# A decoder block with mixed attention and recurrence: narrow score products in pairs, output weights split once, padded value rows, and keys split in two steps

## The chip, the cores and the metric

The kernel runs on one core of one Trainium2 chip. The core has a matrix engine (PE, TensorE, with its weight loads listed apart as PEld), a vector engine (DVE), an activation engine (ACT), a general engine (POOL, GpSimd), a queue engine that starts most DMAs (SP), and 16 DMA engines. Engines run side by side and wait for each other through semaphores; each works through its own instructions in the order in which they stand. The metric is the device time of one execution in microseconds (us), as a median over runs.

## What is computed

One decoder layer over 1024 tokens of width 1024, all in float32. Shortened, with what matters here:

```python
h = h + 0.5 * swiglu(rms_norm(h, ffn1_norm), ffn1_w_gu, ffn1_w_down)
h = h + hybrid_mixer(rms_norm(h, mix_norm), w_in, ..., w_out)
h = h + 0.5 * swiglu(rms_norm(h, ffn2_norm), ffn2_w_gu, ffn2_w_down)
return rms_norm(h, final_norm)

def hybrid_mixer(h, ...):                       # two groups of heads side by side
    o_nsa = nsa_group(...)                      # 8 heads of 64, two key groups
    o_hg = hgrn2_group(...)                     # 4 heads of 128, chunks of 64 tokens
    return concatenate([o_nsa, o_hg]) @ w_out

# hgrn2_group, per chunk and head: a gated linear recurrence
decay = exp(where(tril, b[t] - b[s], NEG))      # b: running sum of log gates
a = einsum('td,tsd,sd->ts', q, decay, k)
o = a @ v + (q * exp(b)) @ state

# nsa_group, per head: three softmaxes with a linear distance penalty, mixed by sigmoid gates
o = g0 * (p_c @ v_c) + g1 * (p_sel @ v_s) + g2 * (p_win @ v_w)
```

`v_c` holds 63 compressed positions per key group; `p_sel` runs over all causal keys (16 blocks of 64 exist and 16 are chosen), `p_win` over a window of 512.

## The kernel before

The float32 products of the dense parts are made of three float32r products: each operand is split into a rounded part and a remainder (`split`, lines 150 to 157: the rounded part on POOL or ACT, the remainder on DVE), and `mm3` (159) or `gemm_tm_steps` (717) multiply high by high, high by low and low by high. Smaller products of the recurrence stay in plain float32; such a product is two passes on PE.

The program goes through these stages, with times from the span's start: the first feed-forward part (0 to about 660 us), the mixer (660 to 1430), the second feed-forward part and the final norm (to the end). A tile framework gives each engine its order and its waits; code that yields (`dense` generators) is interleaved by hand with the rest, so that dense products stand between the dependent steps on PE.

**The recurrence** (`hgrn_unit`, 802, and the loop of `body` at 1406). For each of four heads and two halves of 512 tokens (8 units) the products of one head's two units are interleaved with the projections of the next head (`hgrn_proj`, 769). A unit makes the intra-chunk scores `A` level by level: `score` (811 to 816) multiplies `k` and `q` for four pairs of chunks, 128x128 each, into one PSUM bank; then DVE multiplies parts of `q` and `k` by gate products (832, 833), and the entries that belong to the level are taken over into `A`: the diagonal by a product with the identity (823), levels 0 to 4 by masked copies (837), each for two 64x64 diagonal blocks apart, levels 5 and 6 by copies on ACT (841). That is 8 score rounds per unit, 4 products each. Line 870 multiplies `A` by `v`.

**Compressed keys and values** (`compress`, 902) run in the same stage before the first head's units. `vcm`, the compressed values (977), has 63 rows.

**Attention** (1457 to 1490): for each block of 128 queries (`qb`) and each of two key groups (`g`), `att_soft` (1082) makes, for four heads, scores against the window keys, all keys and the compressed keys (1101, 1102), a minimum of the scaled negative scores by one DVE instruction (1107), exponentials on ACT (1142) and a scaling on POOL (1146). `att_pv` (1150) transposes the probabilities block by block (1175), splits them (1177 on ACT, 1178 on DVE) and multiplies them by the values (1166), the compressed block last, with 63 rows. Dense fillers run beside it: query projections (`att_proj_q`, 1004) in the first half, and in the second half the output product of the first half's tokens (`wout`, 1196). Query projections evacuate their bank in two steps per head pair, ACT (1024) and DVE (1025). `att_kv` (1061) splits the keys of one half for both groups: ACT copies (1078), DVE copies (1079) and DVE subtractions (1080). It is called once before the first half and once before the second (1456).

**The output weights** `w_out` are read in four column quarters (`cq`). `wpages` (301) loads a quarter in four pages and splits each (POOL and DVE); it is called four times in `wout` and once more for the first quarter of the second half's tokens (1485). `wo_pages` (435) does the same for the other three quarters of the second half (1516).

Of the kernel before, what the change touches and what calls it, by code (L numbers as in the profile page):

```python
# [9 lines left out]
F32 = mybir.dt.float32  # L10
# [61 lines left out]
class Net:  # L72
# [15 lines left out]
    def consts(self, ctx):  # L88
# [5 lines left out]
        self.ident = c.tile([128, 128], F32, name="ident")  # L94
        nc.vector.tensor_scalar(self.ident[:], it, 0.0, None, op0=OP.is_equal)
# [205 lines left out]
    def wpages(self, name, key):  # L301

        src = self.wsrc(name, key)
        h, l = [], []
        for kp in range(4):
            raw = self.ap.tile([128, 2, 256], F32, name=self.nm("wr"), tag="kr", bufs=4)
            self.nc.sync.dma_start(out=raw[:], in_=src[:, 2 * kp:2 * kp + 2])
            th, tl = (self.qp.tile([128, 2, 256], F32R, name=self.nm("wq"), tag="qa", bufs=16) for _ in range(2))
            self.split(th[:], tl[:], raw[:])
            h += [th[:, 0, :], th[:, 1, :]]  # L310
            l += [tl[:, 0, :], tl[:, 1, :]]
        return h, l

# [120 lines left out]

    def wo_pages(self, pool, cq):

        raw = self.up_raw(pool, "w_out", cq)
        h, l = [], []
        for kp in range(4):
            th, tl = (pool.tile([128, 4, 128], F32R, name=self.nm("wp"), tag="wp", bufs=16)[:].rearrange("p a b -> p (a b)")  # L440
                      .rearrange("p (k c) -> p k c", k=2) for _ in range(2))
            self.split(th, tl, raw[kp // 2][:, kp % 2 * 2:kp % 2 * 2 + 2, :])
            h += [th[:, 0, :], th[:, 1, :]]
            l += [tl[:, 0, :], tl[:, 1, :]]
        return h, l
# [291 lines left out]
    def mixer_consts(self, tp):  # L737
# [10 lines left out]
        nc.vector.tensor_tensor(out=xf, in0=xf, in1=up, op=OP.mult)  # L748
        self.lev = []
        for l in range(5):  # L750
            m = 1 << l
            nc.vector.tensor_scalar(up, xf, float(m), None, op0=OP.is_ge)
            k = c.tile([128, 128], U8, name=f"lev{l}")
# [48 lines left out]
    def hgrn_unit(self, p, t, half, states, mo):  # L802
# [8 lines left out]
        def score():  # L811
            b = self.bank("b")
            for c in range(4):
                s = slice(c * 128, c * 128 + 128)
                mm(b[:, s], k[:, s], q[:, s], start=True, stop=True)  # L815
            return b[:].rearrange("p (c t) -> p c t", c=4)

        blk = [(slice(o, o + 64), slice(None), slice(o, o + 64)) for o in (0, 64)]
        nc.gpsimd.memset(A[64:128, :, 0:64], 0.0)
        b = score()  # L820
        nc.vector.tensor_tensor(out=q[:], in0=q[:], in1=f[:], op=OP.mult)
        for x in blk:
            nc.vector.tensor_tensor(out=A[x], in0=b[x], in1=self.ident[x[0], None, x[2]].to_broadcast([64, 4, 64]), op=OP.mult)
        F, o = f[:], 0
        for l in range(7):
            m = 1 << l
            n = 512 // (2 * m)
            b = score()
# [6 lines left out]
            if m < 32:  # L835
                for x in blk:
# [65 lines left out]
    def compress(self, p, hg, sp, raw):  # L902
# [12 lines left out]
        self.vcm = sp.tile([64, 2, 128], F32R, name="vcm")  # L915
# [22 lines left out]
        for s in range(2):  # L938
# [29 lines left out]
            else:  # L968
# [6 lines left out]
                hi = self.vcm[:63, :, :64]  # L975
                nc.vector.tensor_copy(out=hi, in_=b3)
                nc.vector.tensor_tensor(out=self.vcm[:63, :, 64:], in0=b3, in1=hi.bitcast(F32), op=OP.subtract)
# [83 lines left out]
    def att_kv(self, p, half, pa=None):  # L1061
# [5 lines left out]
        for g in range(2):  # L1067
# [146 lines left out]
def body(ctx, tc, ins, out):  # L1214
# [177 lines left out]
    if True:  # L1392
# [9 lines left out]
        with cw:  # L1402
            with ExitStack() as ch:
                hg = pool(ch, "hg")
                steps = net.compress(ap_, hg, sp, Y["c"])
                for hh in range(5):
# [5 lines left out]
                    for _ in steps:  # L1412
                        next(dense, None)
                    for _ in dense:
                        pass
# [223 lines left out]
```

## Time and profile before

| | |
|---|---|
| median of 3 runs | 2064.36 us (2063.22 to 2068.18) |
| the profiled execution: its time | 2073.11 us |
| the profiled execution: its span, first to last instruction | 2071.4 us |
| mean granted clock of TensorE in it | 0.989 |
| stage 755 to 1000 us (recurrence) | PE busy 243.68 of 245 us |
| stage 1054 to 1376 us (attention) | PE busy 307.26 of 322 us, DVE 262.31 |
| DMA of the whole span | 273.31 MB, mean 132 GB/s |

The rows quoted below are of four kinds. A row of the timeline gives the start, the duration, the engine, the line and operation, the tiles written and read, and, in brackets, how long the engine had been idle and what ended that wait; "x16" stands for 16 like instructions that follow each other. A row of a group gives a line, an engine, an operation, its shapes and its count, then busy time and the mean duration of one in ns, then the idle time in front of it. A row by stretches gives the stretch and its length, the busy time of PE, PEld, DVE, ACT and POOL with their counts, the clock granted to TensorE (1.00 is full), the share of the DMA engines and GB/s. The page's rows give totals. For a product, "128*63 128x64" is a weight load of 63 columns from 128 rows, and 64 columns streamed over 128 rows.

### The profile page before, as it was taken

The page shows a single profiled execution, that of the slowest core. Times are in us where ns is not written, and L with a number is a line of the kernel's source. Part 1 is how long each engine was busy: PE and PEld are TensorE (multiplying, and loading weights), DVE is VectorE, ACT ScalarE, POOL GpSimd, SP SyncE. Part 2 cuts the span into 40 slices and gives each one's busy share as a digit, 9 for nine tenths or more (in the row PEclk, how much of TensorE's full clock was granted, in tenths as well). Part 3 has the DMA queues.
Part 4 walks back from the last instruction along what each step waited for, and adds up shares of the span by engine and source line. Part 5 has one row for each costly group of instructions (what it writes and reads, how often), then busy time and mean ns, then how long its engine had stood idle before and what let it go on. Part 6 is the DMA issues. An engine that isn't in the chain of part 4 may idle for free.

```text
span 2071.4 us, 30307 instructions
## 1 busy us (share of the span) xinstructions
PE 2023.3 (98%) x10382; PEld 1694.9 (82%) x10382; DVE 1454.0 (70%) x2953; ACT 773.8 (37%) x1619; POOL 531.2 (26%) x632
## 2 busy tenths in 40 slices
PE   8999999999999999999999899999999999999998
PEld 6888888887787889989877688788888888887886
DVE  7977778658766655666458888865867777557677
ACT  5533333313324222212267567645433333323233
POOL 2223223223321001000146444521211222113221
PEclk9999999999999999999989999999999999999999
DMA  5346666267664211100100111152436666247663
GB/s 183 117 134 212 201 231 218 72 217 223 214 193 161 69 57 32 31 27 28 39 18 22 31 47 45 43 179 102 137 116 228 211 205 208 86 143 257 208 193 140
DMA packets 143610, 273.31 MB, mean 132 GB/s; under 512 B 16064, under 2 KB 37600, under 8 KB 143456
## 3 DMA queue, kind: packets, MB, share of 16 engines
q1 hardware_dynamic: 137312, 258.25, 38.2%
q10 hardware_dynamic: 6144, 13.12, 1.7%
q8 instruction: 82, 1.34, 0.3%
q14 instruction: 72, 0.59, 0.1%
HBM read 195.30 MB, written 76.02 MB: 131 GB/s over the span
## 4 chain that ended last, share of the span: by engine, by line
PE 83%; DVE 8%; issue 4%; ACT 2%; DMA 1%; POOL 1%; SPq 0%; ACTq 0%; DVEq 0%; POOLq 0%
PE b L161 15%; PE b L163 15%; PE b L162 15%; PE b L671 6%; PE b L669 6%; PE b L670 6%; PE b L1166 3%; PE b L1175 3%; PE b L815 2%; PE b L725 2%; PE b L724 2%; PE b L726 2%; PE b L1102 1%; PE b L1101 1%; DVE P L1107 1%
## 5 line engine op out<-in xcount | busy, mean ns | idle before, releaser
L161 PE MATMUL b<-xT,wp 128*128 128x512 f32 x1196 | 467.7, 391 | 6.9 <-ACT pp L539 5.6
L162 PE MATMUL b<-xT,wp 128*128 128x512 f32 x1196 | 466.3, 390 | 0.0
L163 PE MATMUL b<-xT,wp 128*128 128x512 f32 x1196 | 465.9, 390 | 0.0
L157 DVE TENSOR_TENSOR dw<-dr,dw 128x512 fp32r<-128x512 f32 x308 | 239.4, 817 | 115.0 <-ACT dw L155 107.2
L161 PEld LDWEIGHTS b<-xT,wp 128*128 128x128 f32 x1196 | 225.1, 188 | 56.4 <-issue 6.0
L162 PEld LDWEIGHTS b<-xT,wp 128*128 128x128 f32 x1196 | 225.2, 188 | 47.1 <-DVE xT L352 0.4
L163 PEld LDWEIGHTS b<-xT,wp 128*128 128x128 f32 x1196 | 225.1, 188 | 46.9
L669 PE MATMUL b<-dw,dw 128*128 128x512 f32 x616 | 242.5, 394 | 7.7 <-DVE dw L157 5.9
L671 PE MATMUL b<-dw,dw 128*128 128x512 f32 x616 | 241.0, 394 | 0.6 <-DVE dw L157 0.4
L670 PE MATMUL b<-dw,dw 128*128 128x512 f32 x616 | 240.9, 391 | 0.0
L155 ACT ACTIVATE dw<-dr 128x512 fp32r<-128x512 f32 x154 | 96.6, 630 | 272.2 <-PE b L669 200.8
L153 POOL TENSOR_SCALAR dw<-dr 128x512 fp32r<-128x512 f32 x154 | 112.9, 735 | 297.8 <-PE b L671 207.8
L155 ACT ACTIVATE wp<-ws 128x512 fp32r<-128x512 f32 x148 | 93.3, 632 | 255.7 <-PE b L162 244.6
L1146 POOL TENSOR_SCALAR P<-P,sm,gate 128x64 f32<-128x64 f32 (+8 forms) x192 | 129.3, 687 | 127.2 <-DVE sm L1144 90.3
L669 PEld LDWEIGHTS b<-dw,dw 128*128 128x128 f32 x616 | 116.4, 189 | 35.5 <-issue 10.3
L671 PEld LDWEIGHTS b<-dw,dw 128*128 128x128 f32 x616 | 116.0, 189 | 29.2 <-DVE dw L157 5.2
L157 DVE TENSOR_TENSOR wp<-ws,wp 128x512 fp32r<-128x512 f32 x148 | 110.1, 745 | 40.1 <-ACT wp L155 40.0
L670 PEld LDWEIGHTS b<-dw,dw 128*128 128x128 f32 x616 | 116.5, 189 | 23.6
L155 ACT ACTIVATE wp<-wr 128x512 fp32r<-128x512 f32 x115 | 72.2, 628 | 156.5 <-PE b L162 128.4
L1142 ACT ACTIVATE P<-P,sm 128x64 f32<-128x64 f32 (+8 forms) x192 | 114.7, 599 | 35.1 <-DVE sm L1107 33.2
L460 POOL TENSOR_TENSOR ws<-wr 128x512 f32<-128x512 f32 x37 | 50.3, 1358 | 299.8 <-DVE wp L157 246.6
L157 DVE TENSOR_TENSOR wp<-wr,wp 128x512 fp32r<-128x512 f32 (+1 forms) x155 | 109.7, 715 | 16.5 <-ACT wp L155 14.2
(293 smaller groups left out, 4016.3 us busy)
## 6 DMA issues: line engine op xcount, KB each, us to landing
dr<-hs SPq DMA_DIRECT2D x242, 256.0 KB, 2.9
wr<-in_ffn_w_gu_dram SPq DMA_DIRECT2D x82, 512.0 KB, 4.0
hs<-hk SPq DMA_DIRECT2D x140, 256.0 KB, 3.8
hs<-wd SPq DMA_DIRECT2D x88, 256.0 KB, 2.8
wd<-in_ffn_w_down_dram SPq DMA_DIRECT2D x84, 256.0 KB, 3.4
dr<-in_ffn_w_down_dram SPq DMA_DIRECT2D x62, 256.0 KB, 3.9
wr<-in_w_in_dram SPq DMA_DIRECT2D x18, 512.0 KB, 4.1
wr<-in_w_out_dram SPq DMA_DIRECT2D x20, 256.0 KB, 3.0
```

The costliest lines, as they stand in the source:

```text
L153: nc.gpsimd.tensor_scalar(out=hi, in0=src, scalar1=1.0, scalar2=1.0, op0=OP.mult, op1=OP.mult)
L155: nc.scalar.activation(out=hi, in_=src, func=AF.Copy)
L157: eng.tensor_tensor(out=lo, in0=src, in1=hi.bitcast(F32), op=OP.subtract)
L161: mm(ps, wh, xh, start=first, stop=False, skip_group_check=skip)
L162: mm(ps, wh, xl, start=False, stop=False, skip_group_check=skip)
L163: mm(ps, wl, xh, start=False, stop=last, skip_group_check=skip)
L669: mm(bs[t][:], hl[:, c], dh[:], start=first, stop=False, skip_group_check=True)
L670: mm(bs[t][:], hh[:, c], dh[:], start=False, stop=False, skip_group_check=True)
L671: mm(bs[t][:], hh[:, c], dl[:], start=False, stop=last, skip_group_check=True)
L1142: nc.scalar.activation(out=rng[br], in_=rng[br], func=AF.Exp, scale=-1.0, bias=m, accum_out=st[:, 6 + br:7 + br])
L1146: nc.gpsimd.tensor_scalar(out=rng[br], in0=rng[br], scalar1=st[:, 6 + br:7 + br], scalar2=self.gate[:, qb, h * 3 + br:h * 3 + br + 1], op0 ...
L1166: mm(O[:], v, t[n][:w], start=n + k == 0, stop=n == last and k == 1)
```

## The change

**Scores.** A chunk pair's 128x128 product becomes, for the diagonal and levels 0 to 5, two 64x64 products, one per chunk of 64 tokens, whose outputs go to partitions 0 to 63 and 64 to 127 of one bank, by way of the two halves of the PE columns (`tile_position`). Level 6, which needs the second chunk against the first, is one 64x64 product per pair. The taken-over entries are collected in a tile `B` with 64 columns, the two blocks at once, and copied to `A` after level 5.

```diff
-        def score():
+        def mm64(out, part, a, b):
+            mm(out[part * 64:part * 64 + 64], k[:, a:a + 64], q[:, b:b + 64], start=True, stop=True,
+               tile_position=(0, part * 64), skip_group_check=True)
+
+        def score(last=False):
             b = self.bank("b")
             for c in range(4):
-                s = slice(c * 128, c * 128 + 128)
-                mm(b[:, s], k[:, s], q[:, s], start=True, stop=True)
-            return b[:].rearrange("p (c t) -> p c t", c=4)
+                o = c * 128
+                if last:
+                    mm64(b[:, c // 2 * 64:c // 2 * 64 + 64], c % 2, o, o + 64)
+                else:
+                    for i in range(2):
+                        mm64(b[:, c * 64:c * 64 + 64], i, o + i * 64, o + i * 64)
+            return b[:, :256].rearrange("p (c t) -> p c t", c=4)
...
-            if m < 32:
-                for x in blk:
-                    nc.vector.copy_predicated(out=A[x], mask=self.lev[l][x[0], None, x[2]].to_broadcast([64, 4, 64]), data=b[x])
+            if l < 5:
+                nc.vector.copy_predicated(out=B[:], mask=self.lev[l][:, None, :].to_broadcast([128, 4, 64]), data=b)
+            elif l == 5:
+                for i in (0, 64):
+                    nc.scalar.activation(out=B[i:i + 32, :, 32:64], in_=b[i:i + 32, :, 32:64], func=AF.Copy)
+                for i in (0, 64):
+                    nc.scalar.activation(out=A[i:i + 64, :, i:i + 64], in_=B[i:i + 64], func=AF.Copy)
             else:
-                for i in range(0, 128, 2 * m):
-                    sl = slice(i, i + m), slice(None), slice(i + m, i + 2 * m)
-                    nc.scalar.activation(out=A[sl], in_=b[sl], func=AF.Copy)
+                for i in range(2):
+                    nc.scalar.activation(out=A[0:64, i::2, 64:128], in_=b[i * 64:i * 64 + 64, 0:2, :], func=AF.Copy)
```

On PE, in the recurrence, two units' scores stand between projection products. Before:

```order
L163 MATMUL b_8055<-xT_5701,wl_8046 128x512
L815 MATMUL b_8100<-q_7480,k_7549 128x128 x4
L815 MATMUL b_8110<-q_7618,k_7684 128x128 x4
L161 MATMUL b_8123<-xT_5695,wh_8045 128x512
L162 MATMUL b_8123<-xT_5696,wh_8045 128x512
```

After:

```order
L164 MATMUL b_8250<-xT_5707,wl_8241 128x512
L826 MATMUL b_8307<-q_7605,k_7692 64x64 x8
L826 MATMUL b_8320<-q_7781,k_7853 64x64 x8
L162 MATMUL b_8336<-xT_5701,wh_8240 128x512
L163 MATMUL b_8336<-xT_5702,wh_8240 128x512
```

Sixteen narrow products stand where eight full ones stood, between the same dense products; over the program 480 stand for 256, in 39 runs instead of 37.

**Output weights.** A new generator `wo_split` loads, splits and writes back all 16 pages of `w_out` once, to DRAM, during the recurrence (one step of it at every other step of the units). `wpages` then only loads the split halves, 8 DMAs of 256 KB per quarter instead of 4 loads and 4 splits; `wo_pages` is gone.

```diff
+    def wo_split(self, p, spill):
...
+                nc.sync.dma_start(out=raw.rearrange("p (k c) -> p k c", k=2), in_=src[:, 2 * kp:2 * kp + 2])
+                self.split(hi, lo, raw)
+                yield
+                page = self.wo[cq, kp] = spill.tile([128, 1024], F32, name=self.nm("wo"), tag="wo", bufs=16)
+                nc.sync.dma_start(out=page[:], in_=t[:].bitcast(F32))
+
+    def wpages(self, cq, tile):
...
+            for k, w in ((slice(512, 1024), h), (slice(0, 512), l)):
+                t = tile()
+                self.nc.sync.dma_start(out=t.bitcast(F32), in_=self.wo[cq, kp][:, k])
+                w += [t[:, :256], t[:, 256:]]
```

**Rows padded to 128.** `vcm` gets 128 rows: zeros in rows 0 to 63, the 63 compressed values in rows 64 to 126. The compressed probabilities now lie right behind the window's in `P2`, and the last block takes the 64 columns in front of them along.

```diff
-        blocks += [(1, 640, 63, self.vcm[:63, g, :])]
+        blocks += [(1, (qb + 1 - lo) * 128 - 64, 128, self.vcm[:, g, :])]
```

**Key split in two steps.** For the second half, `att_kv` is called per group, right before that group's first softmax, and the copies that DVE made there are made by ACT.

```diff
-                nc.vector.tensor_copy(out=ka[other, at[s]], in_=r)
+                if half:
+                    nc.scalar.activation(out=ka[other, at[s]], in_=r, func=AF.Copy)
+                else:
+                    nc.vector.tensor_copy(out=ka[other, at[s]], in_=r)
...
-                net.att_kv(kp1, 1, wf)
             for qb in range(4 * half, 4 * half + 4):
                 for g in range(2):
+                    if qb == 4:
+                        net.att_kv(kp1, 1, (g,), wf)
```

On DVE, at the start of the second half (`kr` are the unsplit keys, `ka` and `kl` their parts, `dwin` the window's distances). Before:

```order
L1079 CAST ka_10754<-kr_9209 64x512
L1080 TENSOR_TENSOR kl_10755<-kr_9209,ka_10754 64x512
L157 TENSOR_TENSOR xT_9570<-os_10721,xT_9569 128x2x128
L1025 SCALAR_TENSOR_TENSOR qa_10744<-b_10621,qa_10744 64x512
L1079 CAST ka_10754<-kr_9263 64x512
L1080 TENSOR_TENSOR kl_10755<-kr_9263,ka_10754 64x512
L1025 SCALAR_TENSOR_TENSOR qa_10747<-b_10621,qa_10747 64x512
L1079 CAST ka_10763<-kr_9209 64x512
L1080 TENSOR_TENSOR kl_10764<-kr_9209,ka_10763 64x512
L1079 CAST ka_10763<-kr_9263 64x512
L1080 TENSOR_TENSOR kl_10764<-kr_9263,ka_10763 64x512
L1107 ISA P_2017_10773,sm_10774<-b_10775,dwin 128x512
```

After:

```order
L1109 TENSOR_TENSOR kl_11066<-kr_9520,ka_11065 64x512
L158 TENSOR_TENSOR xT_9881<-os_11032,xT_9880 128x2x128
L1051 SCALAR_TENSOR_TENSOR qa_11055<-b_10932,qa_11055 64x512
L1109 TENSOR_TENSOR kl_11066<-kr_9574,ka_11065 64x512
L1138 ISA P_2055_11075,sm_11076<-b_11077,dwin 128x512
```

The copies are gone from DVE, and the second group's split stands behind the first softmax instruction instead of ahead of it.

**A bank.** The first two query projections use banks of tag "b" instead of "a", the tag from which `att_soft` takes its banks.

```diff
-            dense = net.att_proj_q(qp, lambda i: net.wtile(wp, "w_in", ("q", i)), X, 0, "a", (0, 1))
+            dense = net.att_proj_q(qp, lambda i: net.wtile(wp, "w_in", ("q", i)), X, 0, "b", (0, 1))
```

More of the change, by code (lines that the diff above doesn't have):

```diff
@@ L94, in consts @@
         self.ident = c.tile([128, 128], F32, name="ident")
+        c.tile([128, 16], F32, name="pad")
         nc.vector.tensor_scalar(self.ident[:], it, 0.0, None, op0=OP.is_equal)
@@ L299, in wtile, with wq_tile @@
         return [[t[:, kt] for kt in range(KT)] for t in (h, l)]
-    def wpages(self, name, key):
-        src = self.wsrc(name, key)
+    def wo_split(self, p, spill):
+        nc = self.nc
+        self.wo = {}
+        for cq in range(4):
+            src = self.wsrc("w_out", cq)
+            for kp in range(4):
+                t = p.tile([128, 1024], F32R, name=self.nm("wo"), tag="fl", bufs=2)
+                lo, hi = t[:, :512], t[:, 512:]
+                raw = lo.bitcast(F32)
+                nc.sync.dma_start(out=raw.rearrange("p (k c) -> p k c", k=2), in_=src[:, 2 * kp:2 * kp + 2])
[4 more added lines that the diff above has]
+    def wpages(self, cq, tile):
         h, l = [], []
         for kp in range(4):
[L306 to L311, printed above, removed]
+            for k, w in ((slice(512, 1024), h), (slice(0, 512), l)):
+                t = tile()
+                self.nc.sync.dma_start(out=t.bitcast(F32), in_=self.wo[cq, kp][:, k])
+                w += [t[:, :256], t[:, 256:]]
         return h, l
+    def wq_tile(self):
+        return self.qp.tile([128, 512], F32R, name=self.nm("wq"), tag="qa", bufs=16)[:]
     def gemm_fm(self, ps, w, c0, n, x, half):
@@ L433, in up_simple @@
             self.split(w[0][:, k], w[1][:, k], raw[o][:, k, e * 128:e * 128 + 128])
[L435 to L445, printed above, removed]
     def up_pieces(self, pool, raw):
@@ L748, in mixer_consts @@
         nc.vector.tensor_tensor(out=xf, in0=xf, in1=up, op=OP.mult)
+        self.id64 = c.tile([128, 64], F32, name="id64")
+        for o in (0, 64):
+            r, k = slice(o, o + 64), slice(o, o + 64)
+            nc.vector.tensor_copy(out=self.id64[r], in_=self.ident[r, k])
+            nc.vector.tensor_copy(out=up[r, 64:], in_=xf[r, k])
+        xf, up = up[:, 64:], up[:, :64]
         self.lev = []
@@ L752, in mixer_consts @@
             nc.vector.tensor_scalar(up, xf, float(m), None, op0=OP.is_ge)
-            k = c.tile([128, 128], U8, name=f"lev{l}")
+            k = c.tile([128, 64], U8, name=f"lev{l}")
             nc.vector.scalar_tensor_tensor(out=k[:], in0=xf, scalar=float(2 * m), in1=up,
@@ L827, in hgrn_unit @@
             n = 512 // (2 * m)
-            b = score()
+            b = score(l == 6)
             F2 = F.rearrange("p (n two) -> p n two", two=2)
@@ L914, in compress @@
         self.kcl = sp.tile([128, 2, 64], F32R, name="kcl")
-        self.vcm = sp.tile([64, 2, 128], F32R, name="vcm")
+        self.vcm = sp.tile([128, 2, 128], F32R, name="vcm")
+        nc.gpsimd.memset(self.vcm[:].bitcast(F32), 0.0)
         nc.vector.tensor_scalar(self.kch[:, :, 63], self.ident[:, 0:2], 0.0, None, op0=OP.mult)
@@ L974, in compress @@
                 b3 = b[:63, :128].rearrange("p (g d) -> p g d", g=2)
-                hi = self.vcm[:63, :, :64]
+                hi = self.vcm[64:127, :, :64]
                 nc.vector.tensor_copy(out=hi, in_=b3)
-                nc.vector.tensor_tensor(out=self.vcm[:63, :, 64:], in0=b3, in1=hi.bitcast(F32), op=OP.subtract)
+                nc.vector.tensor_tensor(out=self.vcm[64:127, :, 64:], in0=b3, in1=hi.bitcast(F32), op=OP.subtract)
     def att_proj_kv(self, p, wp, x):
@@ L1059, in att_tables, with att_kv @@
                                 pattern=[[0, 8]], base=-31, channel_multiplier=1, compare_op=OP.is_ge, fill=0.0)
-    def att_kv(self, p, half, pa=None):
+    def att_kv(self, p, half, gs=(0, 1), pa=None):
         nc = self.nc
@@ L1066, in att_kv @@
         ex = slice(512, 576)
-        for g in range(2):
+        for g in gs:
             pb, other = slice(g * 64, g * 64 + 64), slice(64 - g * 64, 128 - g * 64)
@@ L1097, in att_soft @@
         lo = max(0, qb - 4)
+        wc = (qb + 1 - lo) * 128
+        cmp = P2[:, wc:wc + 64]
         def prod(ka, kl):
@@ L1413, in body @@
                         next(dense, None)
+                        n += hh > 0
+                        if n % 2:
+                            next(pages, None)
                     for _ in dense:
@@ L1422, in body @@
                                       for half in range(2)])
+                for _ in pages:
+                    pass
             cq_, ck, ca, cv = (ExitStack() for _ in range(4))
@@ L1515, in body @@
                 if cq < 3:
-                    w2 = net.wo_pages(wu, cq + 1)
+                    w2 = net.wpages(cq + 1, lambda: wu.tile([128, 4, 128], F32R, name=net.nm("wp"), tag="wp", bufs=16)[:].rearrange("p a b -> p (a b)"))
                 else:
```

14 lines of the change are left out of this document (7 added, 7 removed).

## Prediction

> **What bounds the kernel now.** I read the page first, then busy time by stage, then the waits of PE.
>
> ```profile
> span 2071.4 us, 30307 instructions
> PE 2023.3 (98%) x10382; PEld 1694.9 (82%) x10382; DVE 1454.0 (70%) x2953; ACT 773.8 (37%) x1619; POOL 531.2 (26%) x632
> PE 83%; DVE 8%; issue 4%; ACT 2%; DMA 1%; POOL 1%; SPq 0%; ACTq 0%; DVEq 0%; POOLq 0%
> ```
>
> The first line is the span, the second each engine's busy time, the third the chain of waits by engine. PE is busy nearly throughout, so a saving counts if it shortens PE's own work or fills one of its few idle spots. By stage (length, then busy time of PE, PEld, DVE, ACT, POOL, then the granted clock):
>
> ```profile
> 755.00:1000.00 245.00, 243.68 (x1780) 227.41 (x1779) 155.15 (x453) 49.78 (x169) 18.89 (x24) 1.00 0.09 27
> 1000.00:1054.00 54.00, 51.16 (x250) 42.86 (x249) 26.14 (x88) 20.04 (x64) 12.55 (x22) 0.97 0.11 37
> 1054.00:1376.00 322.00, 307.26 (x1762) 246.36 (x1762) 262.31 (x801) 216.93 (x545) 150.41 (x222) 0.96 0.14 44
> 1376.00:1440.00 64.00, 62.13 (x468) 59.30 (x467) 35.89 (x78) 27.92 (x50) 17.09 (x20) 1.00 0.48 165
> ```
>
> The recurrence (first row) is pure PE work with DVE at 63%. Attention (third row) has 14.7 us of idle PE and a clock of 0.96. The change touches these four stages and nothing else, 685 us of the span.
>
> **Part 1, the scores.** What 128x128 scores cost, from the timeline (start, duration, engine, line):
>
> ```profile
> 769.25 0.40 PE L162 MATMUL b<-xT,wh 128*128 128x512 f32 x1
> 769.25 0.19 PEld L163 LDWEIGHTS b<-xT,wl 128*128 128x128 f32 x1
> 769.48 0.39 PE L163 MATMUL b<-xT,wl 128*128 128x512 f32 x1
> 769.71 2.03 PE L815 MATMUL b<-q,k 128*128 128x128 f32 x16
> 771.50 0.47 PE L161 MATMUL b<-xT,wh 128*128 128x512 f32 x1
> 771.82 0.39 PE L162 MATMUL b<-xT,wh 128*128 128x512 f32 x1
> ...
> L815 PE MATMUL b<-q,k 128*128 128x128 f32 x512 | 64.8, 278 | 1.3 <-DVE q L821 0.6 <-DVE k L833 0.4
> ```
>
> A 512-wide product holds PE for 0.23 us (769.25 to 769.48). The scores start at 769.71, and L162 at 771.82 stands 0.23 behind the stream of L161, so PE was back at 771.59: 1.88 us for 16 passes, 0.1175 each (an f32 product is two passes). The 512 passes of the last row are 60.2 us. Afterwards there are 56 + 4 products per unit, 480 in all, 960 passes of 64x64. The nearest operation that the trace has is L972, a 63-column load and 64 columns streamed:
>
> ```profile
> 754.99 0.40 PE L162 MATMUL b<-xT,wh 128*128 128x512 f32 x1
> 755.31 0.53 PEld L972 LDWEIGHTS b<-w,hid 128*63 128x63 f32 x8 [0.37 <-issue]
> 755.91 0.38 PE L815 MATMUL b<-q,k 128*128 128x128 f32 x1
> ...
> L972 PEld LDWEIGHTS b<-w,hid x8: 132/138/138, 755.3 to 755.7; 128*63 128x63 f32 x8
> L1314 PE MATMUL b<-ones,sq 128*128 128x1 f32 x16 | 1.8, 245 | 0.0
> L961 PE MATMUL b<-hid,w 128*64 128x126 f32 x4 | 0.6, 283 | 0.0
> ```
>
> Eight passes fill (0.53 - 0.138) / 7 = 0.056 us each. L1314 (16 passes of one column in 1.8 us) shows that narrowing the streamed side alone gains nothing beside a 128-column load, and L961 (4 in 0.6) that a 64-column load alone gains little beside 126 columns: both must be halved, as here. PE was free at 754.99 + 0.23 = 755.22 and took L815 at 755.91: 0.69 us, of which 8 x 0.056 = 0.45 are passes and 0.24 is entering and leaving the narrow shape. The order has 39 runs of scores now (37 before): 39 x 0.24 = 9.4 us. If the two halves of a pair follow each other, the sum is 960 x 0.056 + 9.4 = 63.2, a loss of 3.0. If they run wholly side by side, 26.9 + 9.4 = 36.3, a gain of 23.9. No row has two column halves at work together. I take -21, nearly all of the overlap: the halves have separate columns and separate output partitions, and the rows at 769.25 show loads and products already overlapping. It is all on the path, since PE is 99% busy there. [...]
>
> DVE has slack, and loses work (40 masked copies instead of 80, 8 products instead of 16).
>
> **Part 2, rows padded to 128.** A product with 63 rows among full ones:
>
> ```profile
> 1150.43 0.40 PE L161 MATMUL b<-xT,wh 128*128 128x512 f32 x1
> 1150.76 0.50 PE L1166 MATMUL b<-pt,vcm 63*128 63x512 f32 x1
> 1151.18 0.19 PEld L162 LDWEIGHTS b<-xT,wh 128*128 128x128 f32 x1 [0.25 <-issue]
> ...
> L1166 PE MATMUL b<-ph,vcm 63*128 63x512 f32 x16 | 8.5, 533 | 0.9 <-ACT ph L1177 0.9
> L1166 PE MATMUL b<-pt,vcm 63*128 63x512 f32 x16 | 8.6, 535 | 0.2 <-DVE pt L1178 0.2
> ```
>
> It starts 0.33 after its predecessor and its successor comes 0.42 later, 0.75 instead of 0.46: 0.29 lost, the drain into and out of another row shape. Padded, the 32 products lose it: -9.3. The transposes keep their 128 streamed columns, and ACT and DVE go by free size: nothing.
>
> **Part 3, the key split at the second half.**
>
> ```profile
> 1155.97 0.58 PE L1101 MATMUL b<-ka,qa 128*128 128x128 f32 x2 [2.02 <-DVE ka L1079]
> 1157.18 0.41 DVE L1079 CAST ka<-kr 64x512 fp32r<-64x512 f32 x1
> 1158.77 0.69 DVE L1080 TENSOR_TENSOR kl<-kr,ka 64x512 fp32r<-64x512 f32 x1
> 1159.49 0.69 DVE L1107 CUSTOM_DVE_ANT_0 P<-b,dwin 128x512 f32<-128x512 f32 x1
> 1160.24 0.42 PE L1101 MATMUL b<-kch,qa 128*128 128x64 f32 x1 [2.29 <-DVE sm L1107]
> ...
> 1157.30:1167.50 10.20, 7.91 (x27) 6.56 (x26) 8.75 (x31) 4.72 (x13) 2.42 (x4) 0.50 0.16 53
> ```
>
> PE waits twice. The first wait ends with g=0's last copy; now ACT makes it, behind three others and a query split, about when DVE did: -0.3. The second ends when DVE reaches the first L1107, after g=1's split (1157.18 to 1159.46). That split now stands behind, and L1107 follows g=0's last subtraction: -2.3. After the waits PE ran 10.2 us at half clock; 7.91 busy would have been 4 at full. If a third of the stretch goes, -1.3. Sum -4. Bounds: nothing and -6.5 (both waits end, full clock). On the costly side, ACT's four copies (0.6 each) and two DVE subtractions (0.69) for g=1 stand among the exponentials of g=0; uncovered, +3.8.
>
> **Part 4, the bank of the first queries.**
>
> ```profile
> 1036.23 0.69 DVE L1025 SCALAR_TENSOR_TENSOR qa<-b,qa 64x512 fp32r<-64x512 f32 x1 [0.66 <-ACT qa L1024]
> 1037.08 0.30 PE L1101 MATMUL b<-ka,qa 128*128 128x128 f32 x1 [2.85 <-DVE qa L1025]
> 1037.80:1041.20 3.40, 3.40 (x9) 2.63 (x8) 1.10 (x4) 1.78 (x3) 0.00 (x0) 0.50 0.00 0
> ```
>
> The first score needs only the first query tile, done long before; it waits for the second tile's evacuation, whose bank it takes over. With that projection in "b" banks it need not, and the wait (2.85) goes with the half-clock stretch behind it (3.40, 1.7 lost): -4.5. Next late is the query projection behind it, whose weights are split by then. I take -4, bounds 0 and -4.5.
>
> **Part 5, the output weights.**
>
> ```profile
> L157 DVE TENSOR_TENSOR wq<-wr,wq 128x512 fp32r<-128x512 f32 x20 | 16.4, 826 | 1.3 <-POOL wq L153 1.3
> wr<-in_w_in_dram SPq DMA_DIRECT2D x18, 512.0 KB, 4.1
> wr<-in_w_out_dram SPq DMA_DIRECT2D x20, 256.0 KB, 3.0
> ```
>
> Attention loses 20 splits (16.4 us of DVE), mostly not on PE's path: -1, bounds 0 and -3. The recurrence gains 16 splits on idle POOL and on DVE, 16 loads and 16 stores on SP, which waits there anyway. The stores wait for DVE, and the projection weights (4.1 us) queue behind them on SP: 0, or +4 if one comes late. The 64 reloads replace 26 loads; a slot comes free some 10 us of PE work before it is needed, a 256 KB load takes 3.0: 0.
>
> **Sum.** -21 - 9.3 - 4 - 4 - 1 = -39.3. The profiled execution took 2073.11, so 2033.8 for one like it; it was 8.75 above the median, 2064.36. I predict the median, 2025.
>
> **Rivals.** (a) The halves of a pair follow one another, so that "in pairs" does not happen: +3.0 in place of -21, 2049. For it: no row shows the overlap. Against: passes, not issue, fill the 0.056. Chance 0.25.
> (b) Slower by the clock: PE busy 0.72 of 3.5 us before 1037.8 was followed by 3.4 us at 0.50:
>
> ```profile
> 1034.30:1037.80 3.50, 0.72 (x5) 0.74 (x6) 2.22 (x3) 1.15 (x2) 0.62 (x1) 1.00 0.46 150
> ```
>
> If half-empty products count as idleness, the recurrence may fall to half clock; a stretch of 3.4 us costs 1.7, so it decides from 23 of about 66 stretches; at all of them, +112, or 2137. Against: dense products of 0.23 us fill most of the time between score runs, and the clock there is 1.00. Chance 0.05.
> (c) Slower by the loads: if a load could not run beside another half's product, a pass would take 0.11 instead of 0.056: 960 x 0.11 + 9.4 = 115, +55, or 2101. [...] The trace disagrees: at 769.25 a load of all rows runs beside a product of all rows. Chance 0.03.
> (d) The order goes wrong elsewhere (late projection weights, waits for reloads) and eats the gain: about 2062. Chance 0.07.
>
> **Chances.** The forecast has 0.6. A measurement of this kernel tells about 0.3% (6 us) from no change. Faster 0.86, same 0.06, slower 0.08. The range reaches down to every term at its best, -23.9 - 9.3 - 6.5 - 4.5 - 3 = -47.2, so 2017, and 4 further: attention's clock of 0.96 is 13 us of 322 lost, 5 of them in part 3, and of the other 8, in stretches that the parts do not name, half may go when the 63-row drains do. Upwards it takes in (a) with parts 3 and 4 half fulfilled, 2054.
>
> **What would show it.** Right: 64x64 scores at about 30 ns a pass with clock 1.00 in the recurrence, no 63-row products, no wait at the first attention score, a shorter one at the second half. Wrong: passes at 56 ns (a), a clock below 1 in the recurrence (b), PE waiting for wh or wq behind a DMA (d).

## The result and the profile after

| | before | after |
|---|---|---|
| median | 2066.27 us (2063.22 to 2068.2, 4 runs) | 2030.49 us (2027.14 to 2032.32, 4 runs) |
| the profiled execution: time, span | 2073.11, 2071.4 us | 2032.32, 2030.5 us |

The ratio is 0.9826, 95% interval 0.9806 to 0.9846: 36 us faster. The prediction was 2025 with a range of 2013 to 2054, so it held, 5 us too low; but three of its five terms were well off, and that what was wrong with them partly cancelled is luck.

One thing belongs here that the diff above left out: the change also puts a tile of 64 bytes per partition behind `ident`.

```diff
         self.ident = c.tile([128, 128], F32, name="ident")
+        c.tile([128, 16], F32, name="pad")
```

The prediction gave it no term. It turned out to be worth about as much as the scores.

The page of the changed kernel, with the three rows that answer to those shown of before:

```profile
span 2030.5 us, 31275 instructions
PE 1985.7 (98%) x10830; PEld 1662.1 (82%) x10830; DVE 1414.9 (70%) x2889; ACT 784.5 (39%) x1647; POOL 517.9 (26%) x617
PE 84%; DVE 7%; issue 3%; ACT 3%; DMA 2%; POOL 1%; ACTq 0%; SPq 0%; DVEq 0%; POOLq 0%
```

PE stays the bound, with 38 us less of busy time. To see where the time went, I cut both spans at the same points of the program. First before, then after (stretch, length, busy time of PE, PEld, DVE, ACT, POOL, granted clock, DMA): first to last score; to the first attention score; to the first output product; to the last one.

```profile
755.90:988.30 232.40, 231.08 (x1687) 215.69 (x1686) 150.09 (x441) 46.91 (x161) 16.89 (x20) 1.00 0.09 26
988.30:1037.10 48.80, 45.95 (x256) 39.86 (x255) 23.71 (x63) 13.79 (x41) 9.69 (x15) 1.00 0.15 49
1037.10:1157.40 120.30, 113.39 (x539) 85.98 (x540) 87.75 (x309) 84.95 (x257) 61.53 (x113) 0.91 0.04 14
1157.40:1386.40 229.00, 221.17 (x1389) 184.96 (x1389) 190.55 (x543) 141.14 (x318) 99.30 (x126) 0.98 0.20 66
```

```profile
756.70:976.00 219.30, 215.57 (x2139) 190.89 (x2137) 133.16 (x405) 54.24 (x181) 28.02 (x35) 0.98 0.24 83
976.00:1022.00 46.00, 46.00 (x262) 40.17 (x258) 22.51 (x62) 13.65 (x44) 9.66 (x14) 1.00 0.09 29
1022.00:1133.00 111.00, 102.95 (x545) 80.70 (x544) 89.61 (x318) 86.89 (x262) 60.62 (x112) 0.99 0.12 39
1133.00:1349.80 216.80, 212.68 (x1385) 183.30 (x1384) 168.60 (x503) 142.33 (x320) 79.10 (x99) 0.99 0.27 88
```

The first score comes 0.8 us later. The recurrence lost 13.1 us, not 21. The stretch before attention lost 2.8, the first half of attention 9.3, the second 12.2, and 4.3 lie behind. So attention and the way to it gave 24 where the prediction had about 18, and the clock of attention's first half rose from 0.91 to 0.99. Before, attention holds five stretches at half clock (from 1037.8, 1061.7, 1075.3, 1106.1 and 1157.3, together 30.7 us); after, one of 6.8. A us at half clock counts as half a us lost, so that is 12 of the 24.

This is one execution against one, and the one of before had a low clock: 0.989 on average, where 31 of the 44 executions of the kernel before that were timed beside the experiments have 0.993 or more. Span times mean clock estimates what an execution would take at full clock. It is 2046 to 2053 us in those 44, on average 2050.4, and 2016 to 2019 in the four of the changed kernel, on average 2017.7. So by this estimate some 33 of the 36 us are not clock; in the two profiled executions it is 30 of 41.

The scores themselves did what was forecast. The timeline after (start, duration, engine, line), and then the groups of all their passes and of the padded blocks' products:

```profile
775.44 0.39 PE L164 MATMUL b<-xT,wl 128*128 128x512 f32 x1
775.75 1.15 PE L826 MATMUL b<-q,k 128*64 128x64 f32 x32
776.84 0.50 PE L162 MATMUL b<-xT,wh 128*128 128x512 f32 x1
777.17 0.39 PE L163 MATMUL b<-xT,wh 128*128 128x512 f32 x1
```

```profile
L826 PE MATMUL b<-q,k 128*64 128x64 f32 x960 | 37.4, 229 | 3.6 <-DVE q L843 3.5
L1197 PE MATMUL b<-ph,vcm 128*128 128x512 f32 x16 | 7.2, 450 | 0.9 <-ACT ph L1208 0.9
L1197 PE MATMUL b<-pt,vcm 128*128 128x512 f32 x16 | 6.9, 430 | 0.5 <-DVE pt L1209 0.4
```

By the prediction's reckoning PE was free at 775.44 + 0.23 = 775.67 and back at 777.17 - 0.23 = 776.94: 1.27 us for 32 passes, where 16 wide ones took 1.88. The single starts, which the view merges, come in pairs, 6 to 7 ns apart within a pair and 51 to 53 between pairs (100 behind the first). The row of L826 also shows what is new: PE waited 3.5 us for `q` there, almost all of it in one place. The chain of waits around that place ("..." stands for rows of 0.1 us or less, without work):

```profile
811.88 2.80 DMA wo<-wo
...
814.70 3.35 DMA wo<-in_w_out_dram
...
818.21 0.63 POOL wo L154
...
818.86 1.51 DVE wo L158
820.37 0.20 DVE g L811
820.57 1.25 DVE q L843
...
821.87 1.98 PE b L826 x32
```

Read it upwards from the end. The scores at 821.87 wait for `q`, which DVE makes; DVE is late because it takes its work in order and stood before the split of an output weight page (`wo`); the page's load had to wait until the store of an earlier page had freed one of the two buffers. PE stood for 3.12 us, and behind that it ran at half clock:

```profile
821.00:827.80 6.80, 5.93 (x41) 4.61 (x41) 5.43 (x9) 0.00 (x0) 1.44 (x3) 0.50 0.58 200
1131.60:1138.40 6.80, 6.58 (x24) 5.72 (x24) 5.44 (x25) 6.04 (x16) 2.39 (x4) 0.50 0.00 0
```

The second row is the only such stretch left in attention. The waits of parts 3 and 4 in the changed kernel, the first attention score and then those of the second half:

```profile
1021.89 0.22 PE L1132 MATMUL b<-ka,qa 128*128 128x128 f32 x1
1129.96 0.61 PE L1132 MATMUL b<-ka,qa 128*128 128x128 f32 x2 [1.65 <-ACT ka L1106]
1131.91 0.80 PE L1132 MATMUL b<-ka,qa 128*128 128x512 f32 x1 [0.22 <-DVE sm L1138]
```

The first has none; the other two were 2.02 and 2.29 us before.

### The profile page after: what moved, and what is told of

Same layout as the page of the kernel before. It is cut to its first block, busy times and chain, and to the rows that moved or that the text cites. A ratio compares the mean times of both kernels' runs of the same rounds, so it can differ in the third digit from the quotient of the medians.

```text
span 2030.5 us, 31275 instructions
## 1 busy us (share of the span) xinstructions
PE 1985.7 (98%) x10830; PEld 1662.1 (82%) x10830; DVE 1414.9 (70%) x2889; ACT 784.5 (39%) x1647; POOL 517.9 (26%) x617
## 4 chain that ended last, share of the span: by engine, by line
PE 84%; DVE 7%; issue 3%; ACT 3%; DMA 2%; POOL 1%; ACTq 0%; SPq 0%; DVEq 0%; POOLq 0%
PE b L162 16%; PE b L164 15%; PE b L163 15%; PE b L675 6%; PE b L677 6%; PE b L676 6%; PE b L1197 3%; PE b L1206 3%; PE b L730 2%; PE b L731 2%; PE b L732 2%; PE b L826 2%; PE b L1132 1%; PE b L1133 1%; ACT P L1173 1%
## 5 line engine op out<-in xcount | busy, mean ns | idle before, releaser
L1209 DVE TENSOR_TENSOR pt<-b,ph 128x512 fp32r<-128x512 f32 x148 | 99.4, 688 | 23.5 <-ACT ph L1208 22.6
```

The source lines that it names most:

```text
L1209: nc.vector.tensor_tensor(out=l[:w], in0=b[:w], in1=h[:w].bitcast(F32), op=OP.subtract)
```

## The experiments

The theory: each part does what it was put at, and part 5, the output weights, takes some 6.5 us of the scores' gain back in the recurrence by making DVE wait for a page. The rivals: the narrow scores make the wait themselves, because what DVE does between two of them becomes the bound; or the attention's gain is mostly clock, so that single parts are worth more or less than their own work.

**Products of one half, then of the other** (`e1_halves_in_turn`).

```diff
-            for c in range(4):
-                o = c * 128
-...
-                    for i in range(2):
-                        mm64(b[:, c * 64:c * 64 + 64], i, o + i * 64, o + i * 64)
+            for i in range(2):
+                for c in range(4):
+                    o = c * 128
+                    if not last:
+                        mm64(b[:, c * 64:c * 64 + 64], i, o + i * 64, o + i * 64)
+...
```

> The changed kernel with the narrow products of a score written in another order: the four of rows 0 to 63 first, then the four of rows 64 to 127, not in turn. Theory: the two products of a pair overlap because they stand next to each other; apart, a pass takes about 0.056 us as a lone one would (the rival of the prediction), the 32 passes of a run about 1.8 us and not 1.27, the recurrence about 20 us longer, the whole about 2050. Rival: the engine overlaps the halves whatever the order they come in; then a run stays at 1.27 us and the time at 2030 (2024 to 2036).

Measured: 2043.08 us (2041.45 to 2045.38), ratio to before 0.9887 (0.9868 to 0.9906), so 12.6 us slower than the changed kernel. Its timeline, and its row by stretches for the whole recurrence:

```profile
778.20 0.39 PE L164 MATMUL b<-xT,wl 128*128 128x512 f32 x1
778.52 1.54 PE L826 MATMUL b<-q,k 128*64 128x64 f32 x32
779.99 0.50 PE L162 MATMUL b<-xT,wh 128*128 128x512 f32 x1
780.33 0.40 PE L163 MATMUL b<-xT,wh 128*128 128x512 f32 x1
```

```profile
756.90:987.50 230.60, 227.25 (x2136) 203.02 (x2135) 134.21 (x405) 54.33 (x181) 27.69 (x35) 0.99 0.23 79
```

The same 32 passes take from 778.20 + 0.23 to 780.33 - 0.23, 1.67 us in place of 1.27, and the recurrence 11.3 us more. So the order counts: theory right in direction, with a little over half of the size. The single starts show why: the lone passes are 54 to 59 ns apart as expected, but where a pass of the other half comes next in order some still pair up. Neither extreme holds; the alternating order makes all of them pairs.

**The narrow scores alone** (`e2_scores_alone`): the kernel before with the new `hgrn_unit` and `mixer_consts`, without the other parts and without the pad.

> The kernel before with the narrow scores alone; rows, key split, bank and output weights as before. Theory: the scores are worth their 21 us and the output weights' pages took some of it back, so the recurrence (first score to last product with v) is about 21 us shorter than before, without a long wait for DVE's q in it, and the time is about 2045 against 2066; attention as before, with its five half-clock stretches. Rival: the narrow scores bring only what the changed kernel shows in the recurrence, 12 to 13 us, since what DVE does between two scores becomes the bound; then about 2053.

Measured: 2065.25 us (2060.61 to 2071.01, 12 runs), ratio 0.9987 (0.9971 to 1.0003): no difference. Yet the recurrence is as short as the theory had it, 211.50 us and PE busy for nearly all of it, so the rival about DVE falls. About as much was lost where nothing had been edited: the first row is the recurrence, the others the first and the second feed-forward part, and behind them the same two stretches of the kernel before.

```profile
766.10:977.60 211.50, 210.91 (x2137) 186.47 (x2137) 122.52 (x390) 54.11 (x181) 16.93 (x20) 1.00 0.10 29
70.00:435.00 365.00, 365.00 (x1580) 295.69 (x1579) 268.84 (x421) 114.35 (x194) 105.42 (x79) 1.00 0.51 168
1430.00:1840.00 410.00, 409.75 (x1787) 331.88 (x1786) 272.99 (x418) 134.18 (x224) 81.09 (x64) 1.00 0.47 154
```

```profile
70.00:435.00 365.00, 364.38 (x1608) 301.44 (x1608) 271.93 (x419) 115.14 (x195) 105.46 (x80) 1.00 0.51 170
1430.00:1840.00 410.00, 408.32 (x1814) 337.72 (x1814) 276.02 (x426) 137.01 (x228) 80.63 (x64) 1.00 0.47 157
```

PE is full and the clock 1.00 in both, but in the same 365 us it does 1580 products and not 1608. It does not wait; each product takes longer. The trace gives start to start, and the built program says where each operand lies in SBUF:

| products | `xT` or `dw` streamed, address modulo 128 | weights, modulo 128 | start to start |
|---|---|---|---|
| `xT`,`wp`; before, after | 64 | 64 | 227 ns |
| `xT`,`wp`; scores alone | 0 | 64 | 233 ns |
| `dw`,`dw`; scores alone | 0 | 0 | 227 ns |

The smaller masks and `id64` together are 64 bytes shorter than the old masks, so what is placed behind them, 64 of the 88 `xT` tiles among it, moved down by 64 bytes, while `wp`, taken from the other end of SBUF, stayed. The other 24 `xT` tiles stayed too. Set against the built program in order, the same trace shows them apart: of the products with `wp`, 2212 whose `xT` lies at 0 have a median of 233 ns and 1332 whose `xT` lies at 64 have 227. The pad in the change makes up for the shift.

**Scores and pad** (`f1_scores_and_pad`): the same with the line of the pad. **No pad** (`f2_no_pad`): the changed kernel without it. **Half a pad** (`f3_pad_32`): the changed kernel with 32 bytes.

```diff
-        c.tile([128, 16], F32, name="pad")
+        c.tile([128, 8], F32, name="pad")
```

> The kernel before with the narrow scores and with the 64-byte tile named pad that the change also puts behind ident, nothing else. In the run with the narrow scores alone the recurrence was 20.9 us shorter, but the feed-forward products of xT with wp started 233 ns apart and not 227. The smaller masks and id64 shift what lies behind them in SBUF by 64 bytes, xT among it; wp lies at the other end and stays. Theory: a moving tile whose address differs from that of its weights by 64 modulo 128 costs 6 ns per product of 512 columns; the pad puts xT back, the products go at 227 ns, and the time is 2045 (2041 to 2049). Rival: the 233 ns belong to that program or that chip and not to the addresses; then 2065 as there.

> The changed kernel without the 64-byte tile named pad, nothing else changed: xT and all else behind ident lie 64 bytes lower, the weights' tiles at the other end of SBUF where they were. Theory: the products of xT with wp and wh go at 233 ns and not 227; some 2500 of them by 6 to 7 ns are 15 to 18 us: 2046 to 2049. Rival: the addresses do not matter; 2030 (2026 to 2035).

> The changed kernel with a pad of 32 bytes in place of 64: xT then lies 32 bytes below its place in the changed kernel, the weights wp as they were. In the kernel without a pad a difference of 64 modulo 128 between xT and its weights cost 6 ns per product of 512 columns. If any difference in phase costs, the products go at 233 ns and the time is 2046 to 2050; if only the step of 64 does, they go at 227 and it is 2030; if a start off a 64-byte boundary costs by itself, they are slower than 233.

Measured: scores and pad 2050.15 us (2047.41 to 2052.92), ratio 0.992 (0.9901 to 0.9939), 15 us faster than the scores without it; no pad 2049.55 us (2046.54 to 2054.36), ratio 0.9915 (0.9895 to 0.9935), 19 us slower than the changed kernel; half a pad 2052.88 us (2 runs), ratio 0.9942. Scores and pad, its first feed-forward part and its recurrence, and then the first feed-forward part with no pad:

```profile
70.00:435.00 365.00, 364.93 (x1610) 301.88 (x1609) 271.90 (x423) 115.48 (x195) 106.48 (x80) 1.00 0.52 170
755.60:968.40 212.80, 212.13 (x2140) 188.79 (x2138) 122.58 (x391) 54.18 (x182) 16.92 (x20) 1.00 0.10 29
```

```profile
70.00:435.00 365.00, 365.00 (x1579) 295.69 (x1579) 268.85 (x421) 114.30 (x194) 105.35 (x79) 1.00 0.51 168
```

The second fence has the same stretch without the pad: 1579 products in place of 1610, and 233 ns again for `xT` at 0 and `wp` at 64. With the pad it is 227. With half a pad (32 and 64) the median is 235 and the mean 233.4, against a mean of 233.3 with 64 bytes between them, while `dw` with `dw`, both at 32, stays at 227. So the theory holds, in a wider form: what costs is that the two operands lie differently modulo 128, by 32 as by 64; at the places tried (0, 32 and 64) it does not matter where both lie, if they lie alike. Why it costs is not shown.

The scores by themselves, with the pad, are worth 16 us of the whole by times, 19.6 in the recurrence by the traces, and 20 by the estimate at full clock (2029.7 against 2049.8 beside it): the rest was lost to the clock, which is 0.989 to 0.993 in the executions with scores and pad. The pad comes to 18 us by that estimate in both pairs (2047.4 and 2029.7; 2036.0 and 2017.7, without one execution whose clock of 0.945 does not go with its time).

**The blocks' 63 rows** (`e3_rows_63`), **the output weights split in attention** (`e4_weights_in_place`), **keys split at once** (`e5_keys_at_once`) and **the bank "a"** (`e6_bank_a`), each the changed kernel with one part put back; of each edit the lines that matter (the keys' second copy is also back on DVE).

```diff
-        blocks += [(1, (qb + 1 - lo) * 128 - 64, 128, self.vcm[:, g, :])]
+        blocks += [(1, (qb + 1 - lo) * 128, 63, self.vcm[:63, g, :])]
...
```

```diff
-            w = self.wpages(cq, self.wq_tile)
+            w = self.wpages("w_out", cq)
...
-                pages, n = net.wo_split(hg, spill), 0
...
```

```diff
...
                 kp1 = pool(cv, "k1", "right")
+                net.att_kv(kp1, 1, (0, 1), wf)
...
-                    if qb == 4:
-                        net.att_kv(kp1, 1, (g,), wf)
```

```diff
-            dense = net.att_proj_q(qp, lambda i: net.wtile(wp, "w_in", ("q", i)), X, 0, "b", (0, 1))
+            dense = net.att_proj_q(qp, lambda i: net.wtile(wp, "w_in", ("q", i)), X, 0, "a", (0, 1))
```

> The changed kernel with the blocks' 63 rows not padded (that part undone). Theory: 32 products at 0.29 us more, so about 9 us slower than the changed kernel, about 2039; the attention's half-clock stretches as in the changed kernel. Rival: the padding also keeps PE above the share of busy time at which the clock falls, so that stretches come back at 1061 to 1109 and the loss is 14 to 20 us, about 2047.

> The changed kernel with the output weights loaded and split in attention, as before (that part undone). Theory: the split of a page in the recurrence makes DVE wait for its load, hence PE's wait of 3.12 us and the half clock behind it (6.8 us at half speed), about 6.5 us together; without the pages this is gone and attention gets back about 1 us or less, so about 5 us faster than the changed kernel, about 2025. Rival: the wait comes from the narrow scores themselves and stays, and attention loses: 2031 to 2036.

> The changed kernel with the keys of the second half split for both groups at once and the second copy on DVE again (that part undone). Theory of the prediction: the second wait of 2.3 us (PE for the first query block's minimum) comes back, the first grows by 0.3 us and some half clock with them: 4 us slower than the changed kernel, 2034 to 2035. Rival: what the waits of the changed kernel's own (1.64 us at 1128 and the half clock of 6.8 us behind it) cost is as much, and the time stays at 2030 (2027 to 2032).

> The changed kernel with the first query projection in the PSUM banks a again (that part undone). Theory of the prediction: the first attention score again waits 2.8 us for a bank, with a half-clock stretch behind it: 4 to 5 us slower than the changed kernel, about 2035. Rival: the wait came from the queue of weight loads or from elsewhere; no change, 2030.

| put back | median us | ratio to before, 95% | slower than the changed kernel | predicted |
|---|---|---|---|---|
| 63 rows | 2041.57 | 0.9882 (0.9862 to 0.9902) | 11.1 | 9.3 |
| output weights | 2033.44 | 0.984 (0.9821 to 0.9859) | 2.9, within the noise | 1 |
| keys at once | 2036.7 | 0.9866 (0.985 to 0.9882) | 6.2 | 4 |
| bank "a" | 2039.22 | 0.9865 (0.9843 to 0.9888) | 8.7 | 4 |

From one session to the next the median of the kernel before moved between 2063.7 and 2067.5, so the differences in the fourth column, which go across sessions, are uncertain by some 3 us. At full clock, by span times clock, the four come to 8.4, 1.1, 1.6 and 4.2 (uncertain by 1 to 2 us). That is close to the prediction's terms without the clock in them, 9.3, 1, 2.6 and 2.85; the rest of the fourth column is clock.

The rows are as predicted, and half-clock stretches did not come back in number (one, at 1046): that rival falls, and no run shows the share of busy time that it supposes. With the bank "a" the wait at the first attention score is back to the digit, 2.85 us, so it was the bank and not the queue of loads:

```profile
1025.16 0.30 PE L1132 MATMUL b<-ka,qa 128*128 128x128 f32 x1 [2.85 <-DVE qa L1051]
```

With the keys at once the second wait is back, 1.20 us and not 2.29, and the stretch behind the two waits is 10.2 us of half clock where the changed kernel has 6.8:

```profile
1130.27 0.58 PE L1129 MATMUL b<-ka,qa 128*128 128x128 f32 x2 [1.80 <-DVE ka L1105]
1134.53 0.42 PE L1129 MATMUL b<-kch,qa 128*128 128x64 f32 x1 [1.20 <-DVE sm L1135]
```

```profile
1131.50:1141.70 10.20, 9.00 (x32) 7.85 (x33) 8.85 (x32) 5.02 (x14) 2.11 (x3) 0.50 0.00 0
```

Two more half-clock stretches of 3.4 us, from 1042.8 and 1083.7, lie ahead of all that this part touches.

The output weights are the case in which a small result hides two large ones. Their recurrence and the second half of their attention, which answer to 219.30 and 216.80 of the changed kernel:

```profile
754.50:967.20 212.70, 212.03 (x2139) 188.72 (x2137) 122.72 (x390) 54.14 (x181) 16.92 (x20) 1.00 0.10 29
1123.20:1346.30 223.10, 216.42 (x1388) 185.60 (x1388) 188.39 (x539) 143.65 (x322) 101.83 (x126) 0.98 0.20 67
```

Without the pages the recurrence is 6.6 us shorter and has no wait of over 0.25 us, which is the theory. But the second half of attention is 6.3 us longer, with 20 us more of DVE, 2.6 more of idle PE and more half clock. I had expected 2025 of this run; it came to 2033, because I had put the second number at 1. The second row holds 9.8 us at half clock, that of the changed kernel 5.4, which makes 2.2 of the 6.3.

**Both halves of a page on POOL** (`e8_pages_on_pool`), **the load a step ahead** (`e7_load_ahead`), and **a step ahead and held to its step** (`e13_pages_spread`: a page's step is also held behind what stands before it on ACT, POOL, DVE and SP) try to keep the 6 us in attention without paying for them in the recurrence.

```diff
-                self.split(hi, lo, raw)
+                self.split(hi, lo, raw, 'pool', 'pool')
```

```diff
-                self.split(hi, lo, raw)
                 yield
+                self.split(hi, lo, raw)
...
-                            next(pages, None)
+                            with net.late():
+                                next(pages, None)
```

The first two lines of the second diff are `e7_load_ahead`; `e13_pages_spread` has all of it.

> The changed kernel with both halves of each output weight page split on POOL, none on DVE. Theory: PE's wait of 3.12 us for q at 818.7 and the half clock behind it come from DVE, which stands in order behind the split of a page whose load is late; without that split on DVE both go, the recurrence is 6.5 us shorter, about 2024. Rival: POOL takes twice as long for a page and delays the projection weights' split, so that PE waits for wh in the recurrence: 2030 or more.

> The changed kernel with a page's load issued one step of the recurrence ahead of its split, the same work otherwise. Theory: PE's 3.12 us for q come from DVE, which stands behind the split of a page that has not landed; with the load a step ahead that wait and the half clock behind it go, the recurrence is 6.5 us shorter: 2024 (2021 to 2027). Rival: the two buffers of a page (load, split, store, then the next load) are what paces the pages, so that the wait only moves to another page: 2030 (2027 to 2034).

> The changed kernel with each page's load one step ahead of its split, and every page held to its own step of the recurrence (behind what stands before it on each engine), so that the 16 pages spread over some 110 us and not over 80. With the load a step ahead alone, PE's wait for q in the recurrence shrank from 3.12 to 1.65 us. Theory: DVE stands behind a page that has not landed because the pages come faster than their two buffers turn over; spread, no page is late, the wait and the half clock behind it go, first score to last score takes 213 us and not 219, and the time is 2024 (2020 to 2027). Rival: what is won there is given back where idle time happens to fall into another stretch of half clock, as with the load ahead alone; 2030 (2027 to 2033) although the recurrence is shorter.

Measured: on POOL 2042.52 us (2039.38 to 2043.74), ratio 0.988 (0.9858 to 0.9902), 12 us slower than the changed kernel. The wait became longer and took another way: POOL, in order too, splits a projection weight (`wh`) behind four pieces of pages (0.62 to 1.29 us each, from 824.83), and DVE waits for that.

```profile
829.79 2.04 DVE L158 TENSOR_TENSOR wl<-wr,wh 128x1024 fp32r<-128x1024 f32 x1 [5.61 <-POOL wh L154]
833.50 1.98 PE L826 MATMUL b<-q,k 128*64 128x64 f32 x32 [5.91 <-DVE q L843]
```

A step ahead: 2030.4 us (2025.3 to 2030.95), ratio 0.9828 (0.9813 to 0.9842), no different. PE's wait shrank to 1.65 us and the recurrence to 214.90, but 2.5 of the 4.4 us were lost again: 1 before the first score, where a half-clock stretch now lies (from 754.0), and the rest behind the recurrence. Held to its step: 2027.1 us (2025.55 to 2030.77), ratio 0.9808 (0.9786 to 0.9831). Its recurrence and the second half of its attention:

```profile
758.30:972.00 213.70, 212.86 (x2138) 189.01 (x2136) 132.76 (x406) 54.15 (x181) 27.98 (x35) 1.00 0.25 85
1128.80:1344.90 216.10, 211.28 (x1386) 181.37 (x1385) 168.66 (x509) 142.76 (x321) 78.97 (x99) 1.00 0.27 89
```

Both are now near the shorter of their two values (212.70 and 216.80), the recurrence without a wait of over 0.25 us. That shows the mechanism, in the recurrence. The times are 3.4 us lower than the changed kernel's, less than two intervals of some 4 us can tell apart; it is the fastest of the versions, but not by a measured margin over the changed kernel.

## Why the prediction was right, and where not

**Part 1, -21: right.** The recurrence by itself lost 19.6 (with the pad) to 20.9 us (without). The halves overlap, the step on which rival (a) had a quarter of the chance: a pair comes every 58 to 59 ns, a lone pass after 54 to 59, so the second half is nearly free. Rival (c) falls with that, and so does (b): the granted clock is 1.00 over the recurrence in the runs without the pages. Beside 16 pairs the 1.27 us hold 0.33 for entering and leaving the narrow shape, which the prediction had at 0.24.

**Part 2, -9.3: right**, 11.1 by times and 8.4 at full clock. The row products went from 533 and 535 ns to 450 and 430. ACT and DVE were no slower for the padding: before, they took 588 and 680 ns for 63 rows and 593 and 686 for 128.

**Part 3, -4, and part 4, -4: right in mechanism, too small.** Leaving them out cost 6.2 and 8.7. The waits are those that the prediction named: the first of part 3 went from 2.02 us to 1.65, the second from 2.29 to 0.22 at most, that of part 4 from 2.85 to none. At full clock the two cost 1.6 and 4.2, so what was mis-sized is the clock: the two terms of 4 had 1.3 and 1.15 us for it, and the two runs lost 4.6 and 4.5. "Half may go" stood only in the range. These losses do not all lie behind the waits named. In the run with the bank "a", four half-clock stretches were there in attention, two of them 25 and 66 us behind the wait that it brought back. The scores alone and the parts put back one by one sum to more than the whole gain, 16.1 + 11.1 + 6.2 + 8.7 + 2.9 = 45 against 36. At full clock the sum is 20 + 8.4 + 1.6 + 4.2 + 1.1 = 35 against 33, so most of the 9 too many is clock, which each version loses in its own places.

**Part 5: the step that failed.** "The recurrence gains 16 splits on idle POOL and on DVE ...: 0, or +4 if one comes late" took the projection weights as the ones in danger, queued on SP. They came in time. The victim was `q`: DVE takes its work in order, and a split put among the recurrence's steps held up all that stood behind it until its page had landed; PE stood 3.12 us for it. I had asked what is queued behind the waiting instruction on SP, and had not asked it of DVE. It cost 6.6. "Attention -1" was wrong in the other direction by nearly as much, -6.3: the 20 splits were "mostly not on PE's path" by the waits that end at `wq`, but DVE was the engine for which PE waited elsewhere.

**What the prediction did not see: the pad.** Without the line the changed kernel took 2049.55, near the end of the range, with every one of my terms as it is. The prediction saw neither that the masks' new size moves `xT` nor that the line puts it back. That the two cancel, and that part 5 was wrong by 6.6 one way and by 5.3 the other, is luck and no merit of the sum.

## What to carry to other kernels

A change of a table's size moved the tiles behind it. After one, compare how many products the untouched stages do in the same time; 1580 for 1608 at full clock and without a wait is what an operand that had moved against its weights looked like here. And before work is moved to an engine with slack, look at what it waits for: on DVE, busy 133 of 219 us in the recurrence, a split that waited for its load delayed the next step, and PE stood 3.12 us. So the load belongs a step ahead (1.65 us were left here), and the steps far enough apart for the buffers to turn over (no wait of over 0.25 was left).

## What the runs showed of the hardware

**The place of the two operands.** In these traces a product of 512 columns starts every 227 ns if the streamed operand and the weights lie alike modulo 128 bytes in SBUF, and every 233 on average (233.3 and 233.4) with 64 or 32 bytes between them. Without the pad some 3050 products lie so by the built program; at 6 ns each that is 18 us, and the times differ by 15 and 19. So how the two lie to each other costs 6 of 233 ns, and what makes it so is not shown.

**The half clock comes in units.** In the traces of before and after, every stretch at half clock but the last of each span is 3.41 us long, or two or three times that (12 stretches, of 3.41, 6.83 and 10.24 us). Their starts agree: in the changed kernel the half clock of 1131.62 begins 310.61 us, or 91 times 3.413, behind that of 821.01. Waits of 1.6 to 1.7 us were followed by half clock, but the same wait not always. In the changed kernel the wait, from the timeline, and the 3.4 us behind it:

```profile
1083.21 0.51 PE L1197 MATMUL b<-ph,vhl 128*128 128x512 f32 x1 [1.69 <-ACT ph L1208]
```

```profile
1083.20:1086.60 3.40, 3.15 (x13) 1.95 (x14) 3.09 (x10) 2.56 (x8) 2.67 (x5) 1.00 0.00 0
```

With the bank "a" the same:

```profile
1089.68 0.49 PE L1197 MATMUL b<-ph,vhl 128*128 128x512 f32 x1 [1.68 <-ACT ph L1208]
```

```profile
1090.98:1094.38 3.40, 3.40 (x10) 2.33 (x8) 3.10 (x9) 1.25 (x4) 2.67 (x5) 0.50 0.00 0
```

One and the same wait cost 1.7 us or 3.4. Counted in units of 3.413 us from the half clock of its trace, it begins 1.1 us into a unit in the first case and 0.4 in the second. So an idle spot had no fixed price here, and what decides it these runs do not settle. A few us between two versions of this kernel can be nothing more than that.
